# A hybrid encoder layer: half of memory's key and value projection in split fp32r instead of native float32

## The chip, the cores and the metric

One core of a Trainium2 chip runs the whole layer in one launch. The metric is the device time of one execution, in microseconds (us). TensorE (PE) does the matrix products, VectorE (DVE) and ScalarE (ACT) the elementwise work, GpSimd (POOL) a few powers of a half, and SyncE (SP) issues most DMAs. Each engine works through its own list of instructions in order.

## What is computed

The layer takes 512 rows x of width 2048 and 256 memory rows of the same width. Three branches (a gated convolution, banded attention, attention to the memory) are merged by gates and projected. The change concerns one product of it, the projection of the normalised memory rows to keys and values:

```python
mkv = rms_norm(mem, mem_norm_g[l]) @ w_mem_kv[l]      # (256, 2048) @ (2048, 1024)
mk, mv = jnp.split(mkv, 2, axis=-1)
...
h = rms_norm(x, norm_g[l])
proj = h @ w_in[l]                                    # follows at once on the engines
```

All data is float32.

## The kernel before

The work of TensorE is a list of steps; step i is one load of weights (256 rows by 512 columns, 512 KB, a tile `raw` from a ring of 12) and the products with it. `run_steps` (lines 123 to 147) writes out the order for all engines: at step i it issues the loads of step i + 6, the subtractions of weight tiles due at i (`adds`), the weight split of step i + 2, the products of step i, what follows them (`post`), and then what `at_step` has hung on step i, in the order in which it was hung on. Every engine keeps this order (class `Engine`, line 40).

Two kinds of products occur. Native float32: TensorE takes float32 operands as they are, in two records for each product of 128x128 by 128x512. Split fp32r: an operand is split into `hi`, its cast to fp32r on ScalarE, and `lo`, the rest, subtracted on VectorE (`split`, line 182; for weights `split_w`, line 186, into a pool of three pairs). Three products hi·hi, hi·lo, lo·hi replace one (`products`, line 197).

Steps 0 to 15 are memory's projection (`kv_steps`, line 413): step 2c + half multiplies rows 256c to 256c + 255 of the weights, columns of keys (half 0) or values (half 1), with the two blocks of 128 memory rows, four products a step, all native. The transposed memory rows stand in `mT`, eight blocks of 128 features in each of two tiles. `mem_piece(t, k4)` (line 357) makes four of these blocks for one row block t: four transposes on TensorE, then one VectorE multiply with the norm's gain out of PSUM. The pieces k4 = 0 to 3 hang on steps -3, 0, 3 and 5 (line 453). The scale of each row is applied later, when the results leave PSUM (`post`, line 431, on ScalarE after steps 14 and 15).

Beside this, the rows of x are made ready: `x_norm(t)` (line 505) hangs on steps 1, 3, 4 and 6 for row blocks 0 to 3 (four squares on ScalarE, a reduction and a few small VectorE operations with one GpSimd power, then four scalings on VectorE and ScalarE in turn); `x_turn(t, k4)` (line 513) transposes quarters of x on the next two steps, and VectorE evicts them. From these, `Blocks H` (line 460) makes seven sums and differences of blocks (A11, A12, A22, S1 to S4) for Strassen's scheme and splits each in two halves (i = 0, 1); lines 525 to 528 say on which steps.

Steps 16 to 43 are the pair `q` (`pair`, line 237): seven products P1, P5, P6, P3, P7, P2, P4 of four steps each, all split fp32r, 12 records a step. P1 needs A11, P5 S1, P6 S2 (steps 24 to 27), P3 S4, P7 S3, P2 A12 (steps 36 to 39), P4 A22. Before each split of a step from P5 on, VectorE subtracts weight tiles (`sub`, line 249). Other pairs follow in the same form.

Large tiles stand in numbered slots of on-chip memory; `S_OF` (line 341) gives A12 the slots 10 and 11, S2 the slots 4 and 5, which `mT` held.

Of the kernel before, what the change touches and what calls it, by code (L numbers as in the profile page):

```python
# [12 lines left out]
F32R = mybir.dt.float32r  # L13
AF = mybir.ActivationFunctionType
ALU = mybir.AluOpType
# [3 lines left out]
P = 128  # L19
D = 2048  # L20
S = 512
MEM = 256
NK = D // P
NT = S // P
NMT = MEM // P
# [3 lines left out]
KB = 2  # L29
# [36 lines left out]
def trunk_layer(ctx: ExitStack, tc, x, mem, gx, gm, w_in, w_kv, bg, cw, hg, relz, w_a, w_b, w_m, w_o, out):  # L66
    nc = tc.nc
    PE, ACT, DVE = Engine(tc, nc.tensor), Engine(tc, nc.scalar), Engine(tc, nc.vector)
# [16 lines left out]
    gm_sb = cst.tile([P, NK], F32, name="gm_sb")  # L85
# [7 lines left out]
    def slot(i, name, shape=(P, 4, S), dtype=F32):  # L93
        return big.tile(list(shape), dtype, tag=f"s{i}", name=name)

    def cell(name, shape=(P, S)):
        return cel.tile(list(shape), F32, tag="c", name=name)
# [7 lines left out]
    def bank(name, shape=(P, S)):  # L105
        return psp.tile(list(shape), F32, tag="ps", name=name)
# [6 lines left out]
    def after(n, fn):  # L113
        seq[0] += 1
        heapq.heappush(later, (clock[0] + n, seq[0], fn))

    def at_step(i, fn):
        at.setdefault(i, []).append(fn)
# [63 lines left out]
    def split(hi, lo, f):  # L182
        ACT.copy(hi, f)
        DVE.tensor_tensor(lo, f, hi.bitcast(F32), op=ALU.subtract)

    def split_w(raw, name):
        hi = wst.tile([P, KB, S], F32R, tag="whi", name=f"whi_{name}")
        lo = wst.tile([P, KB, S], F32R, tag="wlo", name=f"wlo_{name}")
        split(hi, lo, raw)
        return hi, lo  # L190

    def load(src, name):
        raw = raw_tile(f"raw_{name}")
        SP.dma_start(raw, src.rearrange("(k p) n -> p k n", p=P))
        return raw

    def products(banks, w, acts, first, last, cont=False):

        whi, wlo = w
        nt = len(banks)  # L200
        for j in range(KB * nt):

            kk, t = (j % KB, j // KB) if last else (j // nt, j % nt)
            hi, lo = acts(kk, t)
            for i, (l, r) in enumerate(((hi, whi), (hi, wlo), (lo, whi))):
                PE.matmul(banks[t], l, r[:, kk, :], start=first and kk == 0 and i == 0,
                          stop=last and kk == KB - 1 and i == 2, skip_group_check=cont)
# [138 lines left out]
    SP.dma_start(gm_sb, gm)  # L346
    mraw = [slot(8 + t, f"mem{t}") for t in range(NMT)]
    xraw = [slot((13, 12, 3, 2)[t], f"x{t}") for t in range(NT)]
    mT = []

    def first_loads(j):
        for t in range(NMT):
# [4 lines left out]
    def mem_piece(t, k4):  # L357
        if not mT:
            for i in range(2):
                mT.append(slot(4 + i, f"mT{i}", (P, 8, MEM)))  # L360
        pt = bank(f"pt_mem{t}_{k4}", (P, 4, P))
        for j in range(4):
            PE.transpose(pt[:, j, :], mraw[t][:, k4, j * P:(j + 1) * P], ident)
        j = (k4 % 2) * 4
        DVE.tensor_tensor(mT[k4 // 2][:, j:j + 4, t * P:(t + 1) * P], pt,
                          gm_sb[:, 4 * k4:4 * k4 + 4].unsqueeze(2).broadcast_to([P, 4, P]), op=ALU.mult)

    def mem_rstd(t):
        row_rstd(squares(mraw[t], f"mem{t}"), f"mem{t}", rm[t])
# [2 lines left out]
    def heads_out(name, cells, t0, gcol, dst):  # L372

        st = {}
        n = len(cells)

        def sq(i, h2):
            if "ss" not in st:
                st["ss"] = sml.tile([P, 8], F32, tag="ss8", name=f"ss_{name}{t0}")
            for h in (2 * h2, 2 * h2 + 1):  # L380
                ACT.activation(junk[:, :DH], cells[i][:, h * DH:(h + 1) * DH], AF.Square,
                               accum_out=st["ss"][:, 4 * i + h:4 * i + h + 1])

        def rstd():
            st["r"] = rstd_of(st["ss"][:, :4 * n], 4 * n, 1.0 / DH, f"{name}{t0}")

        def scale(i):
            for h in range(4):
                hs = cells[i][:, h * DH:(h + 1) * DH]
                ACT.mul(hs, hs, st["r"][:, 4 * i + h:4 * i + h + 1])  # L390

        def turn(i):
            pt = bank(f"pq_{name}{t0 + i}", (P, 4, P))
            for h in range(4):
                PE.transpose(pt[:, h, :], cells[i][:, h * DH:(h + 1) * DH], ident)
            qt = cell(f"qt_{name}{t0 + i}", (P, 4, P))
            ACT.mul(qt, pt, gcol)
            after(2, lambda: SP.dma_start(dst(t0 + i), qt))

        for i in range(n):  # L400
            task(0.9, lambda i=i: sq(i, 0))
            task(0.9, lambda i=i: sq(i, 1))
        task(2.7, rstd)
        for i in range(n):
            task(1.1, lambda i=i: scale(i))
        for i in range(n):
            task(1.0, lambda i=i: turn(i))
# [5 lines left out]
    def kv_steps():  # L413
        st = {"ps": {}}
        for c in range(NK // KB):
            for half in range(2):
                def do_load(c=c, half=half):
                    st["raw", c, half] = load(w_kv[c * KB * P:(c + 1) * KB * P, half * S:(half + 1) * S], f"kv{half}_{c}")

                def mm(c=c, half=half):  # L420
                    if c == 0:
                        st["ps"][half] = [bank(f"ps_kv{half}_{t}") for t in range(NMT)]
                    for k in range(c * KB, (c + 1) * KB):
                        for t, ps in enumerate(st["ps"][half]):
                            PE.matmul(ps, mT[k // 8][:, k % 8, t * P:(t + 1) * P], st["raw", c, half][:, k % KB, :],
                                      start=k == 0, stop=k == NK - 1)

                s = Step(mm)
                s.loads.append(do_load)
                if c == NK // KB - 1:  # L430
                    def post(half=half):
                        cells = []
                        for t in range(NMT):
                            kv = cell(f"kv{half}_{t}")
                            ACT.mul(kv, st["ps"][half][t], rm[t])
                            cells.append(kv)
                            if half:
                                after(2, lambda t=t, kv=kv: SP.dma_start(v_d[:, HB:, t, :], kv.rearrange("p (h d) -> p h d", d=DH)))
                        if not half:
                            after(7, lambda: heads_out("mk", cells, 0, hg_sb[:, 3:4],  # L440
                                                   lambda t: mk_d[:, :, t * P:(t + 1) * P]))
                    s.post.append(post)
                steps.append(s)

    kv_steps()

    for j in range(1, 4):
# [3 lines left out]
        steps[1 + i // 2].loads.append(lambda i=i: piece(xraw[i // 4], x, i // 4, i % 4))  # L451

    for k4 in range(4):
        at_step((-3, 0, 3, 5)[k4], lambda k4=k4: [mem_piece(t, k4) for t in range(NMT)])
    for t in range(NMT):
        at_step(9 + t, lambda t=t: mem_rstd(t))
    at_step(5, lambda: DVE.tensor_scalar_mul(qg, hg_sb, float(DH) ** -0.5))
# [65 lines left out]
        at_step(b + 1, lambda t=t: [x_turn(t, 0), x_turn(t, 1)])  # L523
        at_step(b + 2, lambda t=t: [x_turn(t, 2), x_turn(t, 3)])
    for i in range(2):
        for n, what in ((5 + i, "A11"), (7 + i, "A12"), (9, "s1"), (9, "s3"), (10, "S3"), (11, "S1"), (12, "s2"),
                        (12, "s4"), (17 + 2 * i, "S2"), (21 + 2 * i, "S4"), (27 + 3 * i, "A22")):
            at_step(n, lambda i=i, what=what: H.do(what, i))

    def w_pair(src, c0, c1=None):  # L530
# [219 lines left out]
    for u in range(len(units)):  # L750
        i = n_g + EVERY * u
# [181 lines left out]
```

## Time and profile before

| | us |
|---|---|
| median of 3 runs | 1508.66 (1508.45 to 1508.77) |
| profiled execution | 1506.83 |
| its span, first to last instruction | 1505.0 |
| TensorE busy | 1483.8 (99%) |
| VectorE busy | 1146.7 (76%) |
| ScalarE busy | 707.4 (47%) |

The profile shows one execution. Rows in order of time give the start, the time taken, the instruction with output and inputs, how many like it follow one another, and in brackets how long the engine had been idle and what it waited for. An instruction may start before the one ahead of it has ended, so the time from start to start is often shorter than the duration. Helpers record every instruction on one line (L48), so the names of the tiles tell them apart.

### The profile page before, as it was taken

How to read it: one execution, taken by the hardware profiler on the slowest of the kernel's cores; microseconds unless marked ns; L12 is line 12 of the kernel's file. 1: busy time of each engine (PE TensorE's matmuls, PEld its weight loads, DVE VectorE, ACT ScalarE, POOL GpSimd, SP SyncE). 2: the span in 40 equal slices, each digit the busy share in tenths (PEclk: the TensorE clock that was granted, in tenths of full speed). 3: DMA queues.
4: the chain of work that ended last, by engine and by line, in shares of the span. 5: the costliest groups of instructions: out<-in, count | busy, mean ns of one | idle time of the engine just before them, and what ended most of it. 6: DMA issues, size and time to landing. Idle time of an engine off the chain costs nothing.

```text
span 1505.0 us, 17896 instructions
## 1 busy us (share of the span) xinstructions
PE 1483.8 (99%) x6696; PEld 1200.1 (80%) x6696; DVE 1146.7 (76%) x1393; ACT 707.4 (47%) x1102; POOL 22.0 (1%) x23
## 2 busy tenths in 40 slices
PE   8999999999999999999999999999999999998998
PEld 4478888788888888888888888888887888886887
DVE  3887778677888778887877778787887464479977
ACT  3566666543445465444444444444445343354442
POOL 0000000000000000000000000000000000000000
PEclk9999999999999999999999999999999999999999
DMA  9525354363336253626446362543736666410724
GB/s 327 191 66 180 110 175 133 102 215 112 120 90 209 70 196 98 199 89 210 140 144 221 106 223 89 184 150 114 255 133 229 234 218 209 129 43 21 253 83 133
DMA packets 139190, 233.45 MB, mean 155 GB/s; under 512 B 9824, under 2 KB 35680, under 8 KB 138464
## 3 DMA queue, kind: packets, MB, share of 16 engines
q1 hardware_dynamic: 130320, 215.41, 43.7%
q10 hardware_dynamic: 8784, 16.91, 3.4%
q8 instruction: 52, 0.85, 0.2%
q14 instruction: 34, 0.28, 0.1%
HBM read 198.73 MB, written 36.17 MB: 156 GB/s over the span
## 4 chain that ended last, share of the span: by engine, by line
PE 90%; DVE 6%; ACT 1%; DMA 1%; issue 1%; POOL 0%; SPq 0%; DVEq 0%; ACTq 0%; POOLq 0%
PE ps_wb L48 6%; PE psY_gb L48 4%; PE psY_ga L48 4%; PE psY_o L48 4%; PE psY_gm L48 3%; PE ps_kv L48 3%; PE psZ_gm L48 3%; PE psZ_gb L48 3%; PE ps_wa L48 3%; PE ps_wm L48 3%; PE psZ_ga L48 3%; PE psY_k L48 2%; PE psY_cx L48 2%; PE psZ_o L48 2%; PE psY_mqz L48 2%; PE psY_bz L48 2%
## 5 line engine op out<-in xcount | busy, mean ns | idle before, releaser
L48 ACT CAST whi_o_P<-raw_o 128x1024 fp32r<-128x1024 f32 x56 | 58.8, 1054 | 85.1 <-PE psY_o L48 20.2
L48 DVE TENSOR_TENSOR wlo_gb_P<-raw_gb,whi_gb_P 128x1024 fp32r<-128x1024 f32 x56 | 68.2, 1223 | 31.7 <-ACT whi_gb_P L48 31.4
L48 DVE TENSOR_TENSOR wlo_ga_P<-raw_ga,whi_ga_P 128x1024 fp32r<-128x1024 f32 x56 | 68.2, 1223 | 30.9 <-ACT whi_ga_P L48 30.5
L48 DVE TENSOR_TENSOR wlo_gm_P<-raw_gm,whi_gm_P 128x1024 fp32r<-128x1024 f32 x56 | 68.4, 1223 | 23.2 <-ACT whi_gm_P L48 23.2
L48 DVE TENSOR_TENSOR wlo_o_P<-raw_o,whi_o_P 128x1024 fp32r<-128x1024 f32 x56 | 68.3, 1223 | 20.4 <-ACT whi_o_P L48 20.1
L48 ACT ACTIVATE p<-p,nm 128x128 f32<-128x128 f32 (+3 forms) x32 | 18.0, 564 | 107.5 <-DVE nm L48 100.9
L48 ACT CAST whi_gm_P<-raw_gm 128x1024 fp32r<-128x1024 f32 x56 | 58.7, 1051 | 20.8 <-PE psV_gm L48 5.0
L48 ACT CAST whi_ga_P<-raw_ga 128x1024 fp32r<-128x1024 f32 x56 | 58.2, 1049 | 11.4 <-PE psY_az L48 2.8
L48 ACT CAST whi_gb_P<-raw_gb 128x1024 fp32r<-128x1024 f32 x56 | 58.4, 1049 | 6.6 <-PE psY_gb L48 2.0
L48 ACT COPY p<-ptp 128x256 f32<-128x256 f32 (+3 forms) x48 | 19.6, 409 | 88.0 <-PE ptp L48 88.0
L48 PE MATMUL ps_kv<-raw_kv,mT 128*128 128x512 f32 x128 | 59.0, 615 | 1.0 <-DMA raw_kv<-in_w_kv 1.0
L48 PE MATMUL ps_wb<-whi_wb,yb_hi 128*128 128x512 f32 x128 | 50.1, 391 | 0.0
L48 PE MATMUL ps_wb<-whi_wb,yb_lo 128*128 128x512 f32 x128 | 49.8, 389 | 0.0
L48 PE MATMUL ps_wb<-wlo_wb,yb_hi 128*128 128x512 f32 x128 | 49.8, 389 | 0.0
L48 ACT CAST whi_cx_P<-raw_cx 128x1024 fp32r<-128x1024 f32 x28 | 29.5, 1055 | 42.9 <-PE psY_cx L48 13.2
L48 DVE TENSOR_TENSOR wlo_wb<-raw_wb,whi_wb 128x1024 fp32r<-128x1024 f32 x16 | 19.6, 1223 | 38.6 <-ACT whi_wb L48 38.6
L48 PEld LDWEIGHTS ps_kv<-raw_kv,mT 128*128 128x128 f32 x128 | 24.6, 198 | 29.3 <-issue 27.9
L48 DVE TENSOR_TENSOR wlo_cx_P<-raw_cx,whi_cx_P 128x1024 fp32r<-128x1024 f32 x28 | 34.3, 1224 | 17.6 <-ACT whi_cx_P L48 15.9
L48 DVE TENSOR_TENSOR wlo_mqz_P<-raw_mqz,whi_mqz_P 128x1024 fp32r<-128x1024 f32 x28 | 34.3, 1224 | 14.2 <-ACT whi_mqz_P L48 14.2
L48 DVE TENSOR_TENSOR wlo_v_P<-raw_v,whi_v_P 128x1024 fp32r<-128x1024 f32 x28 | 34.1, 1222 | 14.2 <-ACT whi_v_P L48 13.9
L48 ACT CAST whi_mqz_P<-raw_mqz 128x1024 fp32r<-128x1024 f32 x28 | 29.4, 1051 | 31.4 <-PE psZ_mqz L48 10.0
L48 ACT CAST whi_bz_P<-raw_bz 128x1024 fp32r<-128x1024 f32 x28 | 29.5, 1054 | 30.8 <-PE psZ_bz L48 7.7
(658 smaller groups left out, 4684.7 us busy)
## 6 DMA issues: line engine op xcount, KB each, us to landing
raw_ga<-in_w_in SPq DMA_DIRECT2D x32, 512.0 KB, 4.8
raw_gb<-in_w_in SPq DMA_DIRECT2D x32, 512.0 KB, 5.3
raw_gm<-in_w_in SPq DMA_DIRECT2D x32, 512.0 KB, 5.2
raw_o<-in_w_o SPq DMA_DIRECT2D x32, 512.0 KB, 6.2
raw_kv<-in_w_kv SPq DMA_DIRECT2D x16, 512.0 KB, 7.7
raw_q<-in_w_in SPq DMA_DIRECT2D x16, 512.0 KB, 3.8
raw_k<-in_w_in SPq DMA_DIRECT2D x16, 512.0 KB, 4.8
raw_v<-in_w_in SPq DMA_DIRECT2D x16, 512.0 KB, 4.6
```

The costliest lines, as they stand in the source:

```text
L48: ins = getattr(self.engine, op)(*args, **kwargs)
```

## The change

The second half of memory's projection, c = 4 to 7 (steps 8 to 15), becomes split fp32r. For this, `mem_piece` splits the transposed rows of k4 = 2 and 3 into two new tiles `mS`, right behind the multiply that makes them, and the weights of these steps are split two steps ahead as those of `q` are. `mS` stands in the slots 10 and 11. The fourth memory piece hangs on step 4 instead of 5, A12's splits on steps 16 and 17 instead of 7 and 8, the first half of S2 on 18 instead of 17 and the second on 20 instead of 19.

```diff
@@ -346,7 +346,8 @@
     SP.dma_start(gm_sb, gm)
     mraw = [slot(8 + t, f"mem{t}") for t in range(NMT)]
     xraw = [slot((13, 12, 3, 2)[t], f"x{t}") for t in range(NT)]
-    mT = []
+    mT, mS = [], []
+    SPLIT_FROM = 4
 
     def first_loads(j):
         for t in range(NMT):
@@ -361,9 +362,13 @@
         pt = bank(f"pt_mem{t}_{k4}", (P, 4, P))
         for j in range(4):
             PE.transpose(pt[:, j, :], mraw[t][:, k4, j * P:(j + 1) * P], ident)
-        j = (k4 % 2) * 4
-        DVE.tensor_tensor(mT[k4 // 2][:, j:j + 4, t * P:(t + 1) * P], pt,
-                          gm_sb[:, 4 * k4:4 * k4 + 4].unsqueeze(2).broadcast_to([P, 4, P]), op=ALU.mult)
+        j, ts = (k4 % 2) * 4, slice(t * P, (t + 1) * P)
+        gain = gm_sb[:, 4 * k4:4 * k4 + 4].unsqueeze(2).broadcast_to([P, 4, P])
+        DVE.tensor_tensor(mT[k4 // 2][:, j:j + 4, ts], pt, gain, op=ALU.mult)
+        if 4 * k4 >= 2 * SPLIT_FROM:
+            if not mS:
+                mS.extend(slot(10 + i, f"mS{i}", (P, 8, MEM), F32R) for i in range(2))
+            split(mS[0][:, j:j + 4, ts], mS[1][:, j:j + 4, ts], mT[k4 // 2][:, j:j + 4, ts])
 
     def mem_rstd(t):
         row_rstd(squares(mraw[t], f"mem{t}"), f"mem{t}", rm[t])
@@ -425,7 +430,16 @@
                             PE.matmul(ps, mT[k // 8][:, k % 8, t * P:(t + 1) * P], st["raw", c, half][:, k % KB, :],
                                       start=k == 0, stop=k == NK - 1)
 
-                s = Step(mm)
+                def do_split(c=c, half=half):
+                    st["w", c, half] = split_w(st["raw", c, half], f"kv{half}_{c}")
+
+                def mm3(c=c, half=half):
+                    products(st["ps"][half], st["w", c, half],
+                             lambda kk, t: (mS[0][:, (c * KB + kk) % 8, t * P:(t + 1) * P],
+                                            mS[1][:, (c * KB + kk) % 8, t * P:(t + 1) * P]),
+                             False, c == NK // KB - 1)
+
+                s = Step(mm3, do_split) if c >= SPLIT_FROM else Step(mm)
                 s.loads.append(do_load)
                 if c == NK // KB - 1:
                     def post(half=half):
@@ -451,7 +465,7 @@
         steps[1 + i // 2].loads.append(lambda i=i: piece(xraw[i // 4], x, i // 4, i % 4))
 
     for k4 in range(4):
-        at_step((-3, 0, 3, 5)[k4], lambda k4=k4: [mem_piece(t, k4) for t in range(NMT)])
+        at_step((-3, 0, 3, 4)[k4], lambda k4=k4: [mem_piece(t, k4) for t in range(NMT)])
     for t in range(NMT):
         at_step(9 + t, lambda t=t: mem_rstd(t))
     at_step(5, lambda: DVE.tensor_scalar_mul(qg, hg_sb, float(DH) ** -0.5))
@@ -523,8 +537,8 @@
         at_step(b + 1, lambda t=t: [x_turn(t, 0), x_turn(t, 1)])
         at_step(b + 2, lambda t=t: [x_turn(t, 2), x_turn(t, 3)])
     for i in range(2):
-        for n, what in ((5 + i, "A11"), (7 + i, "A12"), (9, "s1"), (9, "s3"), (10, "S3"), (11, "S1"), (12, "s2"),
-                        (12, "s4"), (17 + 2 * i, "S2"), (21 + 2 * i, "S4"), (27 + 3 * i, "A22")):
+        for n, what in ((5 + i, "A11"), (16 + i, "A12"), (9, "s1"), (9, "s3"), (10, "S3"), (11, "S1"), (12, "s2"),
+                        (12, "s4"), (18 + 2 * i, "S2"), (21 + 2 * i, "S4"), (27 + 3 * i, "A22")):
             at_step(n, lambda i=i, what=what: H.do(what, i))
 
     def w_pair(src, c0, c1=None):
```

## Rows read from the trace of the kernel before

**Rows 1.** Page, busy time by engine (us, share, instructions) and the granted clock of TensorE.

```profile
PE 1483.8 (99%) x6696; PEld 1200.1 (80%) x6696; DVE 1146.7 (76%) x1393; ACT 707.4 (47%) x1102; POOL 22.0 (1%) x23
...
PEclk9999999999999999999999999999999999999999
```

**Rows 2.** Waits of TensorE: who waited for whom, us, times, longest.

```profile
PE psY_q L48 <- DVE wlo_q_P L48: 2.7, 1, 2.7
...
PE psY_k L48 <- DVE wlo_k_P L48: 0.6, 1, 0.6
```

**Rows 3.** TensorE in order of time: start, us, instruction, idle before in brackets.

```profile
4.79 2.04 PE L48 MATMUL pt_mem<-ident,mem 128*128 128x128 f32 x8 [4.79 <-DMA mem<-in_mem]
...
7.84 6.22 PE L48 MATMUL ps_kv<-raw_kv,mT 128*128 128x512 f32 x8 [1.01 <-DMA raw_kv<-in_w_kv]
...
25.95 1.04 PE L48 MATMUL pt_mem<-ident,mem 128*128 128x128 f32 x8
...
31.41 1.06 PE L48 MATMUL pt_x<-ident,x 128*128 128x128 f32 x8
...
38.33 1.32 PE L48 MATMUL pt_x<-ident,x 128*128 128x128 f32 x8 [0.67 <-DVE mT L48]
...
76.08 0.80 PE L48 MATMUL psX_q<-whi_q_P,hA_hi 128*128 128x512 f32 x1
```

**Rows 4.** Chain that ended last, first 120 us: start, us, instruction.

```profile
52.61 24.04 PE ps_kv L48 x56
...
76.64 10.93 PE psX_q L48 x48
...
106.82 5.51 PE psY_q L48 x23
```

**Rows 5.** One stretch: us, busy of PE, PEld, DVE, ACT, POOL, granted clock, DMA share, GB/s.

```profile
26.58:105.55 78.97, 76.72 (x285) 47.57 (x283) 63.85 (x101) 44.68 (x83) 4.41 (x6) 1.00 0.51 172
```

**Rows 6.** VectorE in order of time, columns as in group 3.

```profile
26.58 1.29 DVE L48 TENSOR_TENSOR mT<-pt_mem,gm_sb 128x512 f32<-128x512 f32 x2 [3.02 <-PE pt_mem L48]
...
28.98 0.15 DVE L48 TENSOR_REDUCE ss_x<-ss_x 128x1 f32<-128x4 f32 x1
...
35.01 0.16 DVE L48 TENSOR_REDUCE ss_x<-ss_x 128x1 f32<-128x4 f32 x1 [1.65 <-ACT junk L48]
...
41.24 1.22 DVE L48 TENSOR_TENSOR hA_lo<-hf,hA_hi 128x1024 fp32r<-128x1024 f32 x1
...
48.90 1.22 DVE L48 TENSOR_TENSOR hA_lo<-hf,hA_hi 128x1024 fp32r<-128x1024 f32 x1 [1.42 <-ACT hA_hi L48]
...
54.70 0.15 DVE L48 TENSOR_REDUCE ss_mem<-ss_mem 128x1 f32<-128x4 f32 x1
...
62.15 0.16 DVE L48 TENSOR_TENSOR t_mem<-rm 128x1 f32<-128x1 f32 x1 [0.66 <-POOL rm L48]
...
62.81 2.35 DVE L48 TENSOR_TENSOR hS_lo<-hf,hS_hi 128x1024 fp32r<-128x1024 f32 x2
...
74.90 1.23 DVE L48 TENSOR_TENSOR wlo_q_P<-raw_q,whi_q_P 128x1024 fp32r<-128x1024 f32 x1 [1.54 <-ACT whi_q_P L48]
...
103.72 0.17 DVE L48 TENSOR_TENSOR t_mk<-r_mk 128x8 f32<-128x8 f32 x1 [1.83 <-POOL r_mk L48]
...
105.55 2.48 DVE L48 TENSOR_TENSOR wlo_q_P<-raw_q,whi_q_P 128x1024 fp32r<-128x1024 f32 x2
```

**Rows 7.** ScalarE in order of time.

```profile
22.06 0.61 ACT L48 ACTIVATE junk<-x 128x512 bf16<-128x512 f32 x1
...
22.80 0.63 ACT L48 ACTIVATE junk<-x 128x512 bf16<-128x512 f32 x1
...
73.83 1.04 ACT L48 CAST whi_q_P<-raw_q 128x1024 fp32r<-128x1024 f32 x1
```

**Rows 8.** ScalarE, groups by shape: busy us, mean ns, idle before.

```profile
L48 ACT CAST yb_hi<-pt_yb 128x512 fp32r<-128x512 f32 x8 | 4.7, 587 | 13.8 <-PE pt_yb L48 13.8
```

**Rows 9.** DMA queue of SyncE in order of time.

```profile
29.31 5.83 SPq L48 DMA_DIRECT2D raw_kv<-in_w_kv  x7
```

## The prediction

> **What bounds the kernel now.** I read the page first: TensorE is counted busy for 99% of the span and VectorE for 76% [rows 1]. That alone would say that a cheaper product is a gain. But the change lies wholly in the first 120 us, so I read that stage by itself. Next came the waits of TensorE: in this stage, after the start, it has one wait of note, 2.7 us for `wlo_q`, which is VectorE's half of a weight split [rows 2]. The chain of waits puts it at 106.8 us [rows 4], in step 26 (the third of P6 in the q pair; steps 0 to 15 are memory's projection, q starts at 16). So VectorE, not TensorE, sets the time at which the kernel leaves this stage. After it the next one is 0.6 us [rows 2] until the branch weights begin, and TensorE's order is fixed: what TensorE is late in step 26 it is late at the end. The question is therefore: when does VectorE finish `wlo` of step 26, and when could TensorE be there?
>
> VectorE between its third memory piece (26.58) and that split (105.55) is busy 63.9 of 79.0 us [rows 5], so 15.1 us are free. Its queue runs in program order and so do ScalarE's and TensorE's; I follow the three by the lists of `run_steps`, with the durations of the rows. The same walk with the old lists puts step 16 at 76.2 (trace 76.08) and step 26 at 106.9 (trace 106.82) [rows 3, 4], so it may be used for the new ones.
>
> **Part by part.**
>
> *Products.* Native: 56 records, two for each product, take 24.04 us, 0.86 us a product [rows 4]. An fp32r product of the same shape: 48 take 10.93, 0.228 each, three 0.68 [rows 4]. A step has four products: 3.44 before, 2.73 after. Eight steps save 8 x 0.71 = 5.7 us of TensorE. That three-product form on banks that native products opened is not in the trace; nearest are the q pair's rows (same helper, shape and type), which I take; the other end is the native pace, 3.44 a step, which would cancel the 5.7. In the walk even that end moves the result by only 0.7 us, because TensorE waits in these steps anyway.
>
> *Weight splits, steps 8 to 15.* One ScalarE cast (1.04 us [rows 7]) and one VectorE subtraction each (two in 2.35 us, so 1.14 from start to start [rows 6]): VectorE +9.1 us. They need the weights two steps earlier than the products did. The last seven loads were issued by 35.2 us [rows 9] and the first new split comes up at about 45, so I cost the DMA at nothing; it would need a landing time above 10 us to show. Their buffers come free earlier, and q's loads behind them on the queue gain by that.
>
> *Memory row splits.* Four (two token blocks, k4 = 2 and 3). VectorE adds four subtractions of 128x512. That form from SBUF is not there; the row of a 128x512 multiply gives 0.60 apart (two end after 1.29, one takes 0.69) [rows 6], half of the 1024 form 0.57. I take 0.60: +2.4 us. The cast: between half of 1.04 and 0.75 (a square with its accumulator read, two starts at 22.06 and 22.80 [rows 7]); I take 0.59, the nearest shape [rows 8]. But each is a round trip: VectorE writes `mT`, ScalarE casts, VectorE subtracts, and only then the second token block's `mT` can run. VectorE stands 0.76 us each time: 3.0 us of new waits. And ScalarE now has the two casts in its list ahead of the squares of x1 (k4 = 2) and x2 (k4 = 3, one step earlier than before). In the trace x1's squares begin at 22.06, while ScalarE has nothing else to do [rows 7]; in the new list they stand behind a cast that waits for memory's transposes at 25.95 [rows 3].
>
> *A12 and S2.* A12's two splits leave steps 7 and 8 and come at 16 and 17: 2.3 us of VectorE moved, still ahead of step 26, so nothing of the sum. They take the slots of memory's split rows, so their casts wait on step 15's products; behind them on ScalarE stand the casts of steps 19 and 20. By the walk the cast comes up 2 us after those products end, so the wait is nothing. S2's first half one step later: nothing, VectorE's order round it is full either way. No DMA moves with either.
>
> **The walk.** Third memory piece: VectorE 26.6, two round trips to 29.9, two x0 evictions to 31.2. ScalarE starts x1's squares at 29.8 and ends at 32.8; the reduction comes at 32.8 instead of 28.98 [rows 6], and TensorE starts x1's transposes at 35.1 instead of 31.41 [rows 3], standing 3.2 us (the moved k4 = 3 transposes fill 0.9). Fourth piece: two more round trips to 39.1, x2's squares end at 41.6, reduction at 41.6 instead of 35.01 [rows 6]; TensorE stands 3.7 us and starts x2's transposes at 43.9 instead of 38.33 [rows 3]. From there VectorE is 5.3 late (A11 at 46.5 instead of 41.24, the second half at 54.2 instead of 48.90 [rows 6]). Then three weight splits come in and A12 goes out (+1.1): the first reduction of memory's norm at 61.1 instead of 54.70 [rows 6]. TensorE, 0.7 faster a step, has eaten most of its own delay by the end of step 11 at 65.0, but VectorE's list has s1, s3 (4.6 us) before the split of step 12, done at 68.6: a stand of 3.6. Step 13 waits 2.4 behind S3, step 14 0.7, step 15 3.0 behind s2 and s4 (4.6 us). Step 16 starts at 85.6 instead of 76.08 [rows 3]: 9.5 late. `wlo` of step 17, which stood 1.5 us for ScalarE [rows 6], comes at 83.9 instead of 74.90: 9.0 late. Then A12's 2.3 us come in and VectorE's waits for ScalarE go out; `wlo` of step 26 starts at 115.7 instead of 105.55 [rows 6], TensorE at 116.9 instead of 106.82 [rows 4]. **About 10 us late**, with no room to win it back.
>
> The account beside it: free time before 15.1 [rows 5]; after, 3.0 (round trips) + 2.1 (two waits for squares) + 5 x 0.66 (waits for GpSimd, as at 62.15) + 1.8 (as at 103.72) + 1.5 (A11's cast, as at 48.90) [rows 6] + 1.7 (the cast of step 18, behind the evictions of step 15) = 13.4. So 79.0 + 11.5 - 1.7 = 88.8: +9.8. Unknown durations (0.57 to 0.69 for the small subtraction, 0.52 to 0.75 for the small cast, 0.05 us more for each hand-over) move it between +9.5 and +11. I take +10.
>
> The profiled execution took 1506.83 us, 1505.0 of span and 1.8 outside; the median of the runs, 1508.66, lies 1.8 above it. Forecast: 1516.8 for that execution, **1518.7** against the median.
>
> **Rivals.**
>
> *TensorE's clock falls in the new stands: 12%.* At the start, after 4.8 us without work, eight transposes took 2.04 us, later 1.04, and step 0 took 6.22 for eight records, later 3.44 [rows 3, 4]: half the pace, 1.2 for 2.4 GHz, although the clock's row reads 9 there [rows 1]. After the 2.7 us stand at 106.8 the pace was full, 23 records in 5.51 us [rows 4]. The new stands of 3.2 to 3.9 us lie between. One fall costs the extra seen at the start, 2.8 + 1.0 = 3.8; those before step 15 are mostly hidden behind VectorE, the one ahead of step 26 (3.9 us) counts in full: +13.8, 1522.5. The Trainium skill, "TensorE: Matmul & The Clock Gate", Part 1, says that TensorE idles at the half rate and drops back to it after an idle stretch; by that rule this rival would be the forecast if the stands are long enough, and the trace, with one stand that fell and one that didn't, doesn't settle it.
>
> *The round trips hide: 10%.* If the small casts and the squares cost VectorE nothing new, all free time but GpSimd's waits (3.3 + 1.8) could be filled: 15.1 - 5.1 = 10.0 against 11.5 added, +1.5; half of it filled gives +6.5. Midway +4, 1512.7. Against it: VectorE's subtraction reads what ScalarE casts from what VectorE has just written, and nothing stands between in its list.
>
> *Faster: 6%.* TensorE stays the bound: 5.7 us less, 1503.0. It decides at the split of step 26: VectorE would have to end it by 101.1. For it: VectorE is only 76% busy overall [rows 1]. Against: in this stretch it needs 11.5 us more in 5.7 us less, 17.2 out of 15.1 free ones [rows 5].
>
> *The change doesn't do what it says: 4%.* The three products run at less than q's pace; at half of it (5.5 a step) TensorE becomes the bound of steps 8 to 15 and the walk ends at +22, 1531.
>
> **How the numbers follow.** Forecast 68%, with its own range 1518 to 1520. The 8 in 10 takes in the clock and the hidden round trips: 1512.5 to 1523.5. What a measurement of this kernel tells from no change is about 0.2%, 3 us. Slower by more: 68 + 12 + 4 + half of the hidden round trips, 89%. Within: 5%. Faster: 6%.
>
> **What would show it.** Right: `wlo_kv` as a releaser of TensorE in steps 12 to 15, some 10 us together; x1's and x2's transposes waiting for x; VectorE standing before the four `mS` subtractions; step 16 near 85.6, step 26 near 117 with a stand of 3 to 4 us; nothing else changed after 120 us but the shift. Wrong: step 16 before 80, or no `wlo_kv` among the waits (then VectorE had room), or native-pace matmuls after a stand (then the clock).

## The result, and the profile after

The changed kernel takes 1521.45 us (median of 4 runs, 1519.65 to 1523.94) against 1508.66: a ratio of 1.0088, interval 1.0074 to 1.0102 (the two medians alone give 1.0085). It is slower by 12.8 us. The profiled execution took 1523.16 us with a span of 1521.4, 16.4 above the span before. The time lies in the predicted range, on the predicted side, but above the forecast's own range of 1518 to 1520: 2.8 us above the forecast and 1 us below the rival of the falling clock.

The waits of TensorE after the change, to be held against [rows 2]; the columns are us in total, times, longest:

```profile
PE ps_kv L48 <- DVE wlo_kv L48: 6.9, 4, 3.2
PE pt_x L48 <- DVE x L48: 6.5, 2, 3.4
...
PE psY_q L48 <- DVE wlo_q_P L48: 3.3, 1, 3.3
...
PE psY_k L48 <- DVE wlo_k_P L48: 0.6, 1, 0.6
```

The two upper rows are new, 13.4 us together; the stand before step 26 has grown from 2.7 to 3.3, and what follows is as before (0.6). For `wlo_kv` some 10 us were forecast and 6.9 measured, mostly because step 13 waits 0.4 us instead of the 2.4 walked: step 12, which runs slow (below), takes up that wait. TensorE in order of time, to be held against [rows 3]:

```profile
35.49 1.06 PE L48 MATMUL pt_x<-ident,x 128*128 128x128 f32 x8 [3.10 <-DVE x L48]
36.39 3.60 PE L48 MATMUL ps_kv<-raw_kv,mT 128*128 128x512 f32 x8
...
44.31 1.89 PE L48 MATMUL pt_x<-ident,x 128*128 128x128 f32 x8 [3.44 <-DVE x L48]
45.99 4.50 PE L48 MATMUL ps_kv<-raw_kv,mT 128*128 128x512 f32 x8
...
70.98 0.50 PE L48 MATMUL ps_kv<-wlo_kv,mS 128*128 128x512 f32 x1 [3.22 <-DVE wlo_kv L48]
...
85.37 0.79 PE L48 MATMUL ps_kv<-wlo_kv,mS 128*128 128x512 f32 x1 [2.87 <-DVE wlo_kv L48]
...
89.57 0.39 PE L48 MATMUL psX_q<-whi_q_P,hA_hi 128*128 128x512 f32 x1
```

The last row is the start of step 16: 89.6, where 85.6 was forecast.

VectorE in order of time, to be held against [rows 6]:

```profile
28.19 0.69 DVE L48 TENSOR_TENSOR mS<-mT,mS 128x512 fp32r<-128x512 f32 x1 [0.69 <-ACT mS L48]
...
33.06 0.16 DVE L48 TENSOR_REDUCE ss_x<-ss_x 128x1 f32<-128x4 f32 x1 [1.00 <-ACT junk L48]
...
41.90 0.16 DVE L48 TENSOR_REDUCE ss_x<-ss_x 128x1 f32<-128x4 f32 x1 [1.00 <-ACT junk L48]
...
46.94 1.22 DVE L48 TENSOR_TENSOR hA_lo<-hf,hA_hi 128x1024 fp32r<-128x1024 f32 x1
...
50.96 1.29 DVE L48 TENSOR_TENSOR hf<-pt_x,gx_sb 128x512 f32<-128x512 f32 x2 [1.67 <-PE pt_x L48]
...
63.25 0.15 DVE L48 TENSOR_REDUCE ss_mem<-ss_mem 128x1 f32<-128x4 f32 x1
...
91.43 1.23 DVE L48 TENSOR_TENSOR wlo_q_P<-raw_q,whi_q_P 128x1024 fp32r<-128x1024 f32 x1 [2.71 <-ACT whi_q_P L48]
...
119.16 1.22 DVE L48 TENSOR_TENSOR wlo_q_P<-raw_q,whi_q_P 128x1024 fp32r<-128x1024 f32 x1
```

The round trip is there (VectorE stands 0.69 us before the subtraction at 28.19, four times in all), the reductions of x1 and x2 come at 33.1 and 41.9 (forecast 32.8 and 41.6), A11 at 46.9 (46.5). Up to here the trace runs 0.3 to 0.4 us behind the walk. Then it falls back: VectorE stands 1.67 us at 50.96 for TensorE's transposes, memory's reduction comes at 63.3 instead of 61.1, and the split of step 26 at 119.2 instead of 115.7. What the walk did not hold is in the stretches below: us, busy time of TensorE, weight loads, VectorE, ScalarE and GpSimd, then the granted clock.

```profile
45.00:50.00 5.00, 5.00 (x14) 2.77 (x13) 4.29 (x6) 4.69 (x11) 0.00 (x0) 0.72 0.41 147
70.00:75.00 5.00, 4.02 (x11) 3.17 (x12) 4.20 (x10) 4.67 (x5) 0.55 (x1) 0.67 0.36 105
85.00:90.00 5.00, 4.63 (x13) 3.72 (x14) 3.73 (x4) 0.92 (x2) 0.00 (x0) 0.66 0.09 25
120.00:125.00 5.00, 4.56 (x11) 3.61 (x12) 3.88 (x4) 3.68 (x10) 0.00 (x0) 0.50 0.01 2
```

The granted clock is 0.50 to 0.72, that is the lower of the two levels (1.2 instead of 2.4 GHz) for most of each stretch, behind the stands before x2's transposes, step 12, step 15 and step 26. Step 6 takes 4.50 us where its like took 3.60. And the chain of waits has step 26 itself, beside [rows 4]:

```profile
120.44 8.25 PE psY_q L48 x23
```

8.25 us for what took 5.51. So the 16.4 us of this execution are 13.6 up to step 26 (120.4 against 106.8) and 2.7 of half-pace products behind it; from there on the two traces are 16.4 apart at every step.

### The profile page after: what moved, and what is told of

Its sections match the earlier page's. It is cut to its first block, busy times and chain, and to the rows that moved or that the text cites. A ratio compares the mean times of both kernels' runs of the same rounds, so it can differ in the third digit from the quotient of the medians.

```text
span 1521.4 us, 17999 instructions
## 1 busy us (share of the span) xinstructions
PE 1487.3 (98%) x6728; PEld 1211.4 (80%) x6728; DVE 1158.6 (76%) x1405; ACT 718.9 (47%) x1114; POOL 22.1 (1%) x23
## 4 chain that ended last, share of the span: by engine, by line
PE 86%; DVE 7%; DMA 3%; ACT 2%; issue 1%; SPq 0%; POOL 0%; DVEq 0%; POOLq 0%; ACTq 0%
PE ps_wb L48 6%; PE psY_gb L48 4%; PE psY_ga L48 4%; PE psY_o L48 4%; PE psY_gm L48 3%; PE psZ_gm L48 3%; PE psZ_gb L48 3%; PE ps_wa L48 3%; PE ps_wm L48 3%; PE psZ_ga L48 3%; PE psY_k L48 2%; PE psY_cx L48 2%; PE psZ_o L48 2%; PE psY_mqz L48 2%; PE psY_bz L48 2%; PE psY_az L48 2%
## 5 line engine op out<-in xcount | busy, mean ns | idle before, releaser
L48 DVE TENSOR_TENSOR wlo_gm_P<-raw_gm,whi_gm_P 128x1024 fp32r<-128x1024 f32 x56 | 68.5, 1223 | 22.8 <-ACT whi_gm_P L48 22.8
L48 DVE TENSOR_TENSOR wlo_k_P<-raw_k,whi_k_P 128x1024 fp32r<-128x1024 f32 x28 | 34.0, 1222 | 12.2 <-ACT whi_k_P L48 12.1
L48 DVE TENSOR_TENSOR wlo_q_P<-raw_q,whi_q_P 128x1024 fp32r<-128x1024 f32 x28 | 34.0, 1222 | 12.0 <-ACT whi_q_P L48 11.9
```

What stands on the lines that cost most here:

```text
L48: ins = getattr(self.engine, op)(*args, **kwargs)
```

## The experiments

**Theory:** VectorE's list sets the time of step 26; the added subtractions, round trips and late squares put it 10 us later, and TensorE's saving falls into stands. **Rivals:** TensorE itself (the mixed accumulation, or its clock alone), ScalarE's casts, the moves of A12 and of the memory piece. Each time stands beside runs of the kernel before on the same chip.

**No low parts.** The twelve subtractions go; the high parts stand in for the low ones.

```diff
-            split(mS[0][:, j:j + 4, ts], mS[1][:, j:j + 4, ts], mT[k4 // 2][:, j:j + 4, ts])
+            ACT.copy(mS[0][:, j:j + 4, ts], mT[k4 // 2][:, j:j + 4, ts])
...
-                    st["w", c, half] = split_w(st["raw", c, half], f"kv{half}_{c}")
...
+                    ACT.copy(hi, st["raw", c, half])
+                    st["w", c, half] = hi, hi
...
```

> The changed kernel without its twelve new subtractions on VectorE (eight of weights, four of memory rows): the low parts are left out and the high part is used in their place, so TensorE's products, ScalarE's casts, the moved steps and the loads stay, and keys and values of the memory are not the reference's. VectorE's list sets the end (the theory): 11.5 us of VectorE and the round trips go, the walk of the three lists ends 0.2 us below the kernel before, 1508.5, with up to 4 us more if TensorE's clock falls in a stand that is left: 1508 to 1512. Rival, TensorE itself (products slower in the mixed accumulation, or the clock by itself): TensorE's work is as in the changed kernel, 1517 or more. Rival, ScalarE's casts ahead of the squares of x: they stay, 1514 or more.

Measured 1510.24 us, before 1508.09: ratio 1.0014 (1.0004 to 1.0023). 11 of the change's 13 us are gone although TensorE does the same work, ScalarE makes the same casts and the same steps are moved; the rivals' 1514 and 1517 fall. Above the lists' 1508.5 there remain 1.7 us. In the profile the granted clock (third number from the end) falls twice, behind the stands before x2's transposes and step 26:

```profile
40.00:45.00 5.00, 3.91 (x12) 2.39 (x13) 4.83 (x11) 4.51 (x8) 0.00 (x0) 0.66 1.05 388
110.00:115.00 5.00, 5.00 (x17) 4.02 (x16) 2.99 (x4) 3.84 (x8) 0.00 (x0) 0.68 0.23 60
```

That these two falls are the whole rest is likely, but was not tried.

**Rows later.** All the work stays; only the place of four splits changes, and their order: the new `mem_split` makes two casts, then two subtractions.

```diff
-            split(mS[0][:, j:j + 4, ts], mS[1][:, j:j + 4, ts], mT[k4 // 2][:, j:j + 4, ts])
...
+    for k4 in (2, 3):
+        at_step(6, lambda k4=k4: mem_split(k4))
```

> The changed kernel with the four splits of memory's rows hung on step 6 behind x's last norm, the two casts of a piece ahead of its two subtractions. The same work on every engine, so a theory by totals alone expects no change (1521). The theory of the lists: the round trips between VectorE and ScalarE and the late squares of x1 and x2 go (the stands of TensorE before x1's and x2's transposes with them), VectorE is 4.5 us earlier in step 26: 5.5 us above the kernel before, 1514.2, up to 1518 with one fall of the clock.

Measured 1516.04 us, before 1508.09: ratio 1.0053 (1.0038 to 1.0068). TensorE no longer waits for x at all, `wlo_kv` still costs it 8.1 us (five times), and step 26 starts at 114.9 instead of 120.4:

```profile
PE ps_kv L48 <- DVE wlo_kv L48: 8.1, 5, 3.8
...
PE psY_q L48 <- DVE wlo_q_P L48: 2.8, 1, 2.8
```

So about 5 of the 13 us came from where the row splits stood in the lists and in which order, not from how much work they are. What the clock has in these 5 us is not told apart: it falls three times in this profile, before steps 12, 15 and 26 (0.70, 0.50 and 0.66 over 5 us), four times in that of the changed kernel.

**Native products, splits for nothing.**

```diff
-                s = Step(mm3, do_split) if c >= SPLIT_FROM else Step(mm)
+                s = Step(mm, do_split) if c >= SPLIT_FROM else Step(mm)
```

> The changed kernel with all its splits and moves, but the products of steps 8 to 15 native as before, so that the splits of these steps are made for nothing. If TensorE's work counted, it would be 5.7 us slower than the changed kernel, 1527. The theory of the lists: TensorE waits for VectorE anyway, and native steps need no split, so the time is 8.3 us above the kernel before, 1517.0, about that of the changed kernel or a little below; step 26 at 115, stands before x1's and x2's transposes and one before step 16.

Measured 1518.07 us, before 1508.09: ratio 1.0070 (1.0055 to 1.0085), 3 us *below* the changed kernel with 5.7 us more work on TensorE. TensorE's product with `wlo` of step 26 starts at 115.9 (forecast 115), against 120.4 in the changed kernel and 116.9 in the one below whose stands are filled:

```profile
115.92 0.80 PE L48 MATMUL psY_q<-wlo_q_P,hS_hi 128*128 128x512 f32 x1 [3.61 <-DVE wlo_q_P L48]
```

TensorE's saving is worth nothing here; the splits cost 10 us even where nobody reads them. The clock has a part in the 10: it falls twice in this profile, behind the stands before x1's transposes and step 26, and the 23 products from 115.9 on take 8.09 us instead of 5.51.

**The moves alone.**

```diff
-        at_step((-3, 0, 3, 5)[k4], ...
+        at_step((-3, 0, 3, 4)[k4], ...
-        ... (7 + i, "A12"), ... (17 + 2 * i, "S2"), ...
+        ... (16 + i, "A12"), ... (18 + 2 * i, "S2"), ...
```

> The kernel before with the three moves alone (fourth memory piece on step 4, A12 on 16 and 17, S2 on 18 and 20), no split. The theory of the lists: VectorE has the same work ahead of step 26, so 0.6 us below the kernel before at most: 1508.0 (1507 to 1509.5). If moving A12 into the stage where VectorE is full were a cause of its own, 2.3 us above: 1511.

Measured 1507.56 us, before 1508.09: ratio 0.9998 (0.9988 to 1.0008). No cost of their own.

**The clock: the stands filled.** The changed kernel once more, and beside it one with more work on TensorE: ten products that nobody reads in each of four stands.

```diff
+    fill_sb = cst.tile([P, S], mybir.dt.bfloat16, name="fill_sb")
...
+                if i in (12, 15, 26):
+                    fill(i)
                 steps[i].mm()
...
+    def fill(i, n=10):
+        ps = bank(f"ps_fill{i}")
+        for _ in range(n):
+            PE.matmul(ps, fill_sb[:, :P], fill_sb, start=True, stop=True)
...
+        if t == 2:
+            at_step(b + 1, lambda: fill(5))
```

> The changed kernel once more, beside the next one on the same chip: 1519.5 to 1524 as in the result, its runs spread over some 4 us. If a fall of TensorE's clock in the stands makes that spread, the granted clock over steps 6, 12, 15 and 26 differs from execution to execution and no run is below the 1518.7 that the lists give without a fall.

> The changed kernel with ten products of a constant tile, 2.2 us in all, put on TensorE into each of four stands (before x2's transposes, steps 12, 15 and 26); nothing reads them, and they fit into the stands of 2.9 to 3.4 us. If the clock's falls cost what lies above the lists' 10 us, this is FASTER than the changed kernel though TensorE does more: 1518.7, spread under 1 us, granted clock 1.00 throughout. If the clock has no part, it is the changed kernel's time or up to 2 us above it.

Measured 1521.58 us (1521.03 to 1522.48) for the changed kernel and 1516.84 us (1516.74 to 1517.38) for the filled one, before 1508.27: ratios 1.0093 and 1.0062. Doing 40 products more makes it 4.7 us faster (1.9 below the 1518.7 expected) and takes the spread to 0.6 us. In the filled kernel's profile:

```profile
116.89 0.50 PE L48 MATMUL psY_q<-wlo_q_P,hS_hi 128*128 128x512 f32 x1 [1.10 <-DVE wlo_q_P L48]
```

```profile
70.00:75.00 5.00, 2.95 (x13) 2.11 (x12) 4.90 (x8) 3.64 (x4) 0.00 (x0) 1.00 0.37 104
85.00:90.00 5.00, 5.00 (x24) 4.14 (x23) 3.87 (x4) 4.19 (x6) 0.00 (x0) 1.00 0.58 154
120.00:125.00 5.00, 5.00 (x26) 4.12 (x25) 4.25 (x6) 3.65 (x5) 0.00 (x0) 1.00 0.40 115
```

The first fence is TensorE in order of time, the second the stretches with the granted clock, 1.00 in all three. With the clock held, step 26 starts at 116.89, and the span is 1515.1, 10.1 above the span before: the walk of the lists said 116.9, that is +10.1. The points between agree too: the reductions of x1 and x2 come at 32.8 and 41.6, memory's at 61.3, step 16 at 86.0 and the split of step 26 at 115.6, where the walk has 32.8, 41.6, 61.1, 85.6 and 115.7. In the changed kernel's repeat no run is below 1518.7, as expected; the spread was under the 4 us expected (1.5), but its profile shows four falls too (0.54 to 0.75 over 5 us, behind the stands before x1's transposes, step 12, step 15 and step 26). In the filled kernel one is left, 0.69 between 35 and 40 us behind x1's stand, where nothing was filled in; it costs step 26 nothing.

**The keys' norm later, in the kernel before.**

```diff
-                            after(7, lambda: heads_out("mk", ...
+                            after(10, lambda: heads_out("mk", ...
```

> The kernel BEFORE with one edit: the norm of the memory's keys comes three steps later, so that its 2.7 us on VectorE (with the wait of 1.8 us for GpSimd in it) no longer stand ahead of the split of step 26. If VectorE's list sets step 26 in the kernel before too: TensorE's stand of 2.7 us shrinks to under 1, 2.5 us faster than the kernel before, 1506.1. If TensorE were the bound: no change, 1508.6.

Measured 1506.69 us (1506.32 to 1507.06), before 1508.27 (1506.68 to 1509.79): ratio 0.9992 (0.9983 to 1.0001). TensorE's product with `wlo` of step 26 starts at 103.68 instead of 106.82, without a wait:

```profile
103.68 0.50 PE L48 MATMUL psY_q<-wlo_q_P,hS_hi 128*128 128x512 f32 x1
```

So VectorE's list did set step 26 before the change too. But these 3.1 us do not reach the end: the span of the profiled execution is 1504.6 against 1505.0, because TensorE now waits 1.1 us for `wlo` in P3, and 2.6 instead of 1.3 in the pairs k and v. The gain of 1.6 us between the medians (2.5 were expected), at the edge of what the measurement tells, goes mostly with the clock. Each run's mean granted clock is on record: the five runs of the kernel before that have 1.000 take 1506.7 to 1507.2, hardly more than these, and the ten with 0.997 to 0.999 take 1508.2 to 1509.8. That the clock falls there in the one stand of 2.7 us is likely, but no profile of the kernel before shows a fall.

**The low parts on GpSimd.** Rows later, keys' norm later, and the eight weight subtractions on an engine that is idle.

```diff
-                    st["w", c, half] = split_w(st["raw", c, half], f"kv{half}_{c}")
...
+                    ACT.copy(hi, st["raw", c, half])
+                    POOL.tensor_tensor(lo, st["raw", c, half], hi.bitcast(F32), op=ALU.subtract)
...
```

> The changed kernel with memory's rows split on step 6 (as in the run with rows later), the norm of the memory's keys three steps later, and the eight weight subtractions of steps 8 to 15 on GpSimd instead of VectorE. GpSimd's time for 128x1024 is in no trace; its 128x128 select took 0.29 us, eight times that is 2.3, an estimate. By the lists: at 1.2 us each 4.7 below the kernel before, at 2.3 some 2 below (1506.5), at 4.0 GpSimd becomes the bound of steps 8 to 15 and it is 7 above (1516). If VectorE were not the cause, its relief gives nothing against the run with rows later (1516).

Measured 1516.56 us, before 1508.27: ratio 1.0059 (1.0045 to 1.0072), where 1506.5 was expected. Taken by itself this would speak against the theory, since VectorE had 9.1 us less in its list. But it did not get them back. GpSimd and VectorE in order of time over the same stretch:

```profile
58.64 2.40 POOL L48 TENSOR_TENSOR wlo_kv<-raw_kv,whi_kv 128x1024 fp32r<-128x1024 f32 x1
...
68.52 9.55 POOL L48 TENSOR_TENSOR wlo_kv<-raw_kv,whi_kv 128x1024 fp32r<-128x1024 f32 x3 [1.22 <-ACT whi_kv L48]
```

```profile
58.70 2.35 DVE L48 TENSOR_TENSOR t_mem<-rm 128x1 f32<-128x1 f32 x1 [2.62 <-POOL rm L48]
...
67.99 4.51 DVE L48 TENSOR_TENSOR hS_lo<-hf,hS_hi 128x1024 fp32r<-128x1024 f32 x2
72.42 6.73 DVE L48 TENSOR_TENSOR hS_lo<-hf_S,hS_hi 128x1024 fp32r<-128x1024 f32 x2
```

The single one of GpSimd takes 2.40 us, near the estimate of 2.3. But while its three run from 68.5 to 78.1, VectorE's four subtractions take 11.2 us instead of the 4.7 of [rows 6] (two in 2.35), and a multiply of 128x1, 0.16 us elsewhere [rows 6], takes 2.35 at 58.70, just as long as GpSimd's beside it. The two engines take turns. What VectorE loses in these rows, 6.5 and 2.2 us, is about the 9.1 that it was spared. (TensorE's clock falls in this profile too, to 0.56 between 70 and 75 us.) The Trainium skill, "SBUF — State Buffer", section "SBUF: two separate sides", says that a VectorE instruction with two SBUF inputs and a GpSimd instruction that reads SBUF exclude each other for a whole instruction; the trace agrees (2.35 us for the 128x1 multiply beside 2.40).

**Two moves, nothing split; and the smallest dose of the change.**

```diff
# two moves, on the kernel before
-                            after(7, lambda: heads_out("mk", ...
+                            after(10, lambda: heads_out("mk", ...
-        at_step((-3, 0, 3, 5)[k4], ...
+        at_step((-3, 0, 3, 4)[k4], ...
# last quarter, on the changed kernel, with the keys' norm later
-    SPLIT_FROM = 4
+    SPLIT_FROM = 7
+    at_step(9, lambda: mem_split(3))
```

> The kernel BEFORE, all native in memory's projection, with two moves: the norm of the memory's keys three steps later (as in the run with the keys' norm later) and the fourth memory piece on step 4. By the lists 3.7 us below the kernel before: 1504.6 (1504 to 1506.5), step 16 at 75, no stand over 1.2 us, granted clock 1.00 throughout, runs within 1 us. If the gain of the first move alone was all there is: 1506.7.

> The run with two moves plus a smaller dose of the change: only steps 14 and 15 in three fp32r products, memory's last piece split on step 9 (casts ahead of subtractions), A12 and S2 as in the changed kernel. TensorE has 2 x 0.71 = 1.4 us less work than in the run with two moves. If TensorE were the bound: 1503.2. By the lists VectorE's 3.5 us more turn that into a stand ahead of step 15: 2.7 below the kernel before, 1505.6, slower than the run with two moves by 1.

Measured 1505.55 us for the two moves and 1506.52 us for the last quarter, before 1508.09: ratios 0.9984 (0.9975 to 0.9993) and 0.9993 (0.9985 to 1.0002). The two moves beat both kernels, by 2.5 us and 16; the lists gave 3.7. About half of the 2.5 is again the clock: the eight runs of the kernel before beside them that have a mean granted clock of 1.000 have a median of 1506.7, so 1.2 us are left. Three of the expected signs failed: no stand over 1.2 us, a clock of 1.00 throughout, runs within 1 us (they spread over 2.1). In the profiled execution, the slowest of its runs, x0's transposes wait 2.1 us for x and the step behind them takes 5.29 us at a granted clock of 0.73; whether the faster runs have something of it is not shown (their mean granted clock is 0.999 or 1.000, this one's 0.998). And two split steps out of eight already cost 1 us net, as expected: TensorE has 1.4 us less to do and waits 1.7 us before step 15.

```profile
PE ps_kv L48 <- DVE wlo_kv L48: 1.7, 1, 1.7
```

## Why the prediction was right, and where it was off

*What bounds the stage.* Right. VectorE sets step 26: taking its new work away takes 11 us away (no low parts), making TensorE's work longer costs nothing (native with splits: step 26 at 115.9, in the filled kernel at 116.9).

*Products.* Right in size: in the changed kernel 30 records between 60.34 and 67.14 us run 0.227 apart, 2.72 a step, in banks that native products opened. The 5.7 us are real and worth nothing.

*Splits and round trips.* Right: +11.5 us of VectorE were forecast and its busy time grew by 11.9 (1146.7 to 1158.6), four stands of 0.69 (taken at 0.76), the late squares; "rows later" is 8.0 us above its kernel before, the changed kernel 13.3 above its own, so the place and order of the row splits are worth 5.3 us, falls of the clock in both included, where the walk gave 4.5.

*A12 and S2.* Right, nothing.

*The sum of the lists.* Right: +10 was forecast, the filled kernel has +10.1 in its span with step 26 at 116.9 as walked, and is within 0.5 us of the walk at the points between.

*The clock.* This is the step that failed. The prediction took it at nothing, with 12% for one fall at 3.8 us. It fell in both profiled executions of the changed kernel, four times each, and cost 4.7 us between the medians (1521.58 against 1516.84). The prediction had named the sign, native-pace matmuls after a stand. In the profiled execution above it is 16.4 less the lists' 10.1, 6.3 us: 2.7 are step 26's half-pace products (3.8 had been assumed for a fall), the rest came by way of VectorE: x2's transposes and step 6 ran slow and VectorE stood 1.67 us for them, where it does not stand in the filled kernel, and the slow step 15 held up the cast of step 18, for which VectorE stood 2.71 us (at 91.43) instead of 1.13. So the falls that I had called hidden behind VectorE were not wholly hidden, because VectorE's list waits for TensorE's transposes and, through ScalarE's evictions of step 15, for its products. The argument that a stand of 2.7 us had left the pace alone was one row of one execution, and too little to set the chance by.

*The offset of 1.8 us* between the profiled execution and the median was added to the forecast as if it belonged to every run. Most runs of the kernel before have a fall of the clock of their own that the profiled execution did not have: of the 55 runs beside the experiments, 18 have a mean granted clock of 1.000, as the profiled execution, and take 1506.3 to 1507.8 us; the other 37 have 0.997 to 0.999 and take 1507.3 to 1509.9. Beside the filled kernel, the five runs at 1.000 have a median of 1506.8: against them the filled kernel is 10.0 us slower, as the lists say, and the changed kernel 14.8, of which 4.7 go with the clock. So the forecast of 1518.7 was 1.9 too high by the offset and 4.7 too low by the falls left out; that the one took back part of the other is luck.

## What to carry to other kernels

Ask of a cheaper product whether the engine that prepares its operands has room in that very stretch: here TensorE was 99% busy over the kernel, and yet the 5.7 us saved went wholly into stands behind VectorE's 11.5 us of splits. A split that goes to and fro between two in-order engines costs more than its instructions; put all casts ahead of all subtractions, and off the way of what the next stage waits for (5 us here for both; they were not tried one by one). And a stand on TensorE has a second price, its clock: filling it with products that nobody reads was 4.7 us faster. It can be in the kernel that one measures against, too: compare the granted clock of the runs before a difference of 1 or 2 us is put down to work.

## What the runs showed of the hardware that I had not expected

- TensorE's granted clock fell behind stands of 2.9 to 3.4 us in the changed kernel, and in the run without low parts behind one of 2.05 us before x2's transposes (0.50 between 42 and 44 us), while a stand of 3.2 us before step 26 left it at 1.00 in the run with the moves alone. The same stand of 3.1 us before x1's transposes left it at 1.00 in the first profile of the changed kernel and took it to 0.50 in the second; 2.7 us before step 26 left it at 1.00 in the profile of the kernel before and took it to 0.66 (over 5 us) in that second one. So the length of a stand alone does not tell whether the clock falls; what else decides was not tried. The Trainium skill, "TensorE: Matmul & The Clock Gate", Part 1, has the engine at the half rate after an idle stretch; the runs agree with the direction.
- GpSimd's subtraction of 128x1024 float32 takes 2.40 us, and VectorE's two-input instructions stand still while it runs: 11.2 us for four that take 4.7.
- A float32 product of 128x128 by 128x512 in three fp32r records costs 0.68 us against 0.86 native [rows 4]: a fifth less, before the splits are paid for.
